# Chain banks of the first four gate pairs copied whole to SBUF before VectorE adds their halves, and the fifth product in its wide form in every pair

## The chip, the cores and the metric

The kernel runs on one core of one Trainium2 chip. The metric is device time in microseconds (us) of one execution, and the median over several executions is compared. The engines of a core run side by side and each takes its instructions in order: PE (TensorE, matmuls), DVE (VectorE), ACT (ScalarE), POOL (GpSimd, here almost only an issuer of DMAs) and SP (an issuer of DMAs).

## The reference

A decoder trunk of two layers on 512 tokens of width 1024, in float32. Layer 0 mixes tokens with a short gated convolution, layer 1 with sliding-window attention. Both layers end with the same feed-forward block, and the change lies there:

```python
D_MODEL, SEQ, D_FF = 1024, 512, 2816

def swiglu(h, w_gate_up, w_down):
    g, u = jnp.split(h @ w_gate_up, 2, axis=-1)
    return (jax.nn.silu(g) * u) @ w_down

def reference(x, ...):
    h = x
    for l in range(2):
        ...                                   # token mixing of the layer
        ff = swiglu(rmsnorm(h, ffn_pre_norm[l]), ffn_w_gate_up[l], ffn_w_down[l])
        h = h + rmsnorm(ff, ffn_post_norm[l])
    return h
```

## The kernel before

**Precision.** Every float32 operand is split into a high part (`hi`, a copy rounded by ACT) and a low part (`lo = x - hi`, by DVE), and a product is hi·hi + hi·lo + lo·hi on PE. So each weight tile of 128x1024 costs one ACT copy (`whi`, line L479) and one DVE subtraction (`wlo`, L480). Some weight tiles are sums of others that DVE adds first (L467).

**Stages.** The 22 column blocks of 128 of the gate and up matrices are taken in pairs. The first two blocks are computed plainly; the other 20 are ten *gate pairs*, numbered q = 0 to 9. Each pair is a 2x2 block product done with seven products instead of eight, and its jobs run in the order 1, 2, 6, 5, 7, 3, 4. After pairs 2, 4, 6 and 9 a stage of the down projection follows, also in the seven-product form; the first of these, after pair 2, is called down stage 0, and its first three jobs d0, d1 and d2 here.

**Chains.** PSUM has eight banks of 128x512. Products 1, 6, 7 and 4 add up in one pair of banks, the chain X (tile `gx`). After each of them `take` reads the running sum out before the next of the four may write: into `st` after 1, 6 and 4, and added to `u` after 7. Product 5 goes to chain Z (`gz`), product 2 to Y (`gy`), product 3 to Z as well or to a bank V of its own (`gv`).

**Wide and narrow.** A wide product has one 128x512 matmul for hi·(hi and lo) and one 128x256 matmul for lo·hi in each step, so each of its two banks holds two halves that must still be added: the first half by an ACT copy of 128x256, the second by a DVE addition that reads PSUM. A narrow product has three 128x256 matmuls in each step and one bank. Before, product 5 is narrow in pairs 0 and 1 (`FIVE = 2`), where it shares the one bank of Z with product 3, and wide from pair 2 on.

**Order.** The jobs stand in one list. After job j has been issued, `in_line` prepares job j + 3: ACT's `whi`, then DVE's `wlo`. So on DVE and ACT the reading-out of a product, the splitting of weights for three jobs later, and the splitting of the activations of the pair before (`s`, `ahi`, `alo`, L590 to L601) alternate in one fixed order:

```python
        for j, job in enumerate(jobs):
            if job.run:
                job.run(job)            # PE's matmuls, then take()
            prepare(j + LINE_LEAD)      # LINE_LEAD = 3: whi, wlo, then the sum for j + 4
            ...
                    late.pop(0)()       # a piece of the activations' splitting
            late += job.then() or [] if job.then else []   # after product 3: ACT's Silu
```

Gate pairs 0 to 2 and down stage 0 have no other work between them.

Of the kernel before, what the change touches and what calls it, by code (L numbers as in the profile page):

```python
# [12 lines left out]
AF = mybir.ActivationFunctionType  # L13
# [28 lines left out]
WARM = 9  # L42
LEAD = 2
LINE_LEAD = 3
FIVE = 2

EARLY_IN, REST_IN = 2, 0
ORDER = (
# [27 lines left out]
def yoco_kernel(  # L76
# [22 lines left out]
    nc = tc.nc  # L99
# [15 lines left out]
    def name(s):  # L115
        uid[0] += 1
        return f"{s}_{uid[0]}"

    def slot(s, dt=F32, w=S):
        return big.tile([P, w], dt, tag="slot", name=name(s), padded_shape=[P, S])  # L120

    def wide(s, dt=F32):
        return wides.tile([P, D], dt, tag="wide", name=name(s))
# [7 lines left out]
    def bank(s, pool=None):  # L131

        if pool is None:
            pool = (ps_mm, ps_sc, ps_mm, ps_pt)[turn[0] % 4]
            turn[0] += 1
        return pool.tile([P, S], F32, tag="bank", name=name(s))
# [56 lines left out]
    def mm3(out, whi, wlo, xhi, xlo, start, stop, **kw):  # L193
        nc.tensor.matmul(out, whi, xlo, start=start, stop=False, **kw)  # L194
        nc.tensor.matmul(out, whi, xhi, start=False, stop=False, **kw)  # L195
        nc.tensor.matmul(out, wlo, xhi, start=False, stop=stop, **kw)  # L196
# [256 lines left out]
    class Job:  # L453
# [10 lines left out]
        def add(self):  # L464
            if self.make:
                raw = self.raws[0].tile
                nc.vector.tensor_tensor(out=raw, in0=raw, in1=self.raws[1].tile, op=ALU.add)  # L467
# [203 lines left out]
    with tc.manual_schedule(engines=ALL):  # L671
# [52 lines left out]
        v = small.tile([P, 4], F32, tag="v", name=name("v"))  # L724
# [15 lines left out]
    both = []  # L740
# [84 lines left out]
    with tc.manual_schedule(engines=ALL):  # L825
# [21 lines left out]
        pools = {"p": ps_pt, "m": ps_mm, "s": ps_sc}  # L847
# [134 lines left out]
    def ffn(l, before, ahead, gain, gpres, following):  # L982
# [20 lines left out]
        def gate_jobs(q, factors, out, to, then):  # L1003

            sums = sums_of[f"g{l}{q}"]
            a21, a22, a11, a12 = (Raw(b) for b in sums.blocks)
            s1, s3, *rest = (Raw(b) for b in sums.sums)
            raws = {1: [a11], 2: [a12], 5: [s1], 7: [s3], 4: [a22]}  # L1010
            if rest:
                raws[6], raws[3] = ([r] for r in rest)
            else:
                raws[6], raws[3] = [a11, s1], [a12, a11]
            five = q >= FIVE
            broad = "XZ" if five else "X"
            chain = {1: "X", 6: "X", 7: "X", 4: "X", 5: "Z", 3: "V" if five else "Z", 2: "Y"}
            pools = {"X": ps_mm, "Y": ps_pt, "V": ps_pt, "Z": ps_sc}
            split = {}
            if q == 0:  # L1020

                pools = {"X": ps_sc, "Y": ps_pt, "V": ps_pt, "Z": ps_mm}
                raws[1], raws[2] = [], []
                split = {1: ahead.ready[4], 2: ahead.ready[5]}
            banks, kept = {}, []

            def tiles(a):
                return a.rearrange("p (e c) -> p e c", e=2)

            def take(p):  # L1030
                x, y, z, v = (banks.get(c) for c in "XYZV")
                st, u, gr = kept
                g0, g1 = (gr.rearrange("p (e h c) -> p e h c", e=2, h=2)[:, :, h]
                          for h in range(2))

                def add(out, a, b):
                    nc.vector.tensor_tensor(out=out, in0=a, in1=b, op=ALU.add)  # L1037

                if p == 2:
                    add(g0, tiles(y), tiles(st))  # L1040
                elif p == 5:
                    if not five:
                        nc.scalar.activation(u, z, AF.Copy)
                        return
                    for e in range(2):
                        ue = u[:, e * 256 : (e + 1) * 256]
                        nc.scalar.activation(ue, z[e][:, :256], AF.Copy)
                        add(ue, z[e][:, 256:], ue)
                    add(st, u, st)
                elif p == 3:  # L1050
                    add(g1, tiles(v if five else z), tiles(st))
                else:
                    for e in range(2):
                        a, b = x[e][:, :256], x[e][:, 256:]
                        ste, ue = (v[:, e * 256 : (e + 1) * 256] for v in (st, u))
                        if p == 7:
                            add(ue, a, ue)
                            add(ue, b, ue)
                            continue
                        nc.scalar.activation(ste, a, AF.Copy)  # L1060
                        add(ste, b, ste)
                if p == 4:
                    for g, m in ((g0, st), (g1, u)):
                        nc.vector.scalar_tensor_tensor(out=g, in0=tiles(m), scalar=-1.0, in1=g,
                                                       op0=ALU.mult, op1=ALU.mult)

            def run(p):
                def products(job):
                    if not kept:
                        kept.extend([slot("st"), slot("st"), wide("gr")])  # L1070
                    whi, wlo = split[p] if p in split else job.w
                    c = chain[p]
                    opened = c not in banks
                    if opened:
                        banks[c] = ([bank("g" + c.lower(), pools[c]) for _ in range(2)]
                                    if c in broad else bank("g" + c.lower(), pools[c]))
                    steps = [(e, k, slice(e * S + k * P, e * S + (k + 1) * P))
                             for e in range(2) for k in range(4)]
                    kw = {"skip_group_check": True}
                    if c in broad:  # L1080
                        for e, k, kk in steps:
                            nc.tensor.matmul(banks[c][e], whi[:, kk], factors[p][k][2],  # L1082
                                             start=opened and k == 0, stop=False, **kw)
                        for e, k, kk in steps:
                            nc.tensor.matmul(banks[c][e][:, :256], wlo[:, kk], factors[p][k][0],  # L1085
                                             start=False, stop=k == 3 and p in (4, 5), **kw)
                    else:
                        for e, k, kk in steps:
                            mm3(banks[c][:, e * 256 : (e + 1) * 256], whi[:, kk], wlo[:, kk],
                                *factors[p][k][:2], opened and e == k == 0,  # L1090
                                e == 1 and k == 3 and p in (2, 3), **kw)
                    take(p)
                return products

            def gate():
                nc.scalar.activation(kept[2], kept[2], AF.Silu)  # L1096

            def end():
                late = out(kept[2], to)
                then()  # L1100
                return late

            return [Job(raws[p], run(p), {3: gate, 4: end}.get(p), len(raws[p]) > 1)
                    for p in (1, 2, 6, 5, 7, 3, 4)]
# [42 lines left out]
        with tc.manual_schedule(engines=ALL):  # L1147
# [5 lines left out]
            def then(hf, k):  # L1153
                if hf == 0 and k in (5, 6):
                    for b in ((0, 1), (2, 3))[k - 5]:
                        before.turn(b, (2,))
                if hf == 0 and k == 6:
                    for b in range(4):
                        before.turn(b, (3,))
                    for f in range(KT):  # L1160
                        before.split(0, f, 1)
                    for b in range(4):
                        before.keep(b, 1)
                if hf == 1 and k == 1:
                    factors.update(before.factors())
                if hf == 1 and k == 3:
                    sum_on(f"{l}f0")
# [10 lines left out]
            for rd, (f0, f1) in enumerate(ROUNDS):  # L1178
                last = rd == len(ROUNDS) - 1
                for f in range(max(f0, PLAIN), f1, 2):  # L1180
                    q = (f - PLAIN) // 2
# [135 lines left out]
    class Heads:  # L1317
# [115 lines left out]
        def out(self):  # L1433
            if self.t < BOTH:
                hi, lo = halves("ohl", F32R)
            else:
                hi, lo = slot("ohi", F32R), slot("olo", F32R)
            nc.scalar.activation(hi, self.po, AF.Copy)
            nc.vector.tensor_tensor(out=lo, in0=self.po, in1=hi.bitcast(F32), op=ALU.subtract)
            at.append((hi, lo))  # L1440
# [25 lines left out]
    with tc.manual_schedule(engines=ALL):  # L1466
# [20 lines left out]
        for hf in range(2):  # L1487
            c = slice(hf * 256, (hf + 1) * 256)
# [54 lines left out]
    with tc.manual_schedule(engines=ALL):  # L1543
        sum_on("a0")
        for i in range(KT + 2):
# [9 lines left out]
            for c in order.split():  # L1555
# [11 lines left out]
                if op == "g":  # L1567

                    u = 2 * (t - EARLY - 1) + n[0]
# [126 lines left out]
```

## Time and profile before

| | |
|---|---|
| median of 3 runs | 1015.99 us (1015.88 to 1016.23) |
| the profiled execution | 1015.87 us, span 1014.1 us |
| granted TensorE clock | 0.999 |
| PE busy | 1005.4 us, 99% |
| DVE busy | 888.1 us, 88% |
| ACT busy | 582.6 us, 57% |
| gate pairs 0, 1, 2 of layer 0 (at us) | 204.0, 223.8, 243.5; down stage 0 from 263.8 |
| the same of layer 1 | 701.5, 721.1, 740.9; down stage 0 from 761.3 |

The timeline and the stretches give microseconds from the start of the span. A row of the timeline has start, duration, engine, line, operation, output and inputs, and at its end in square brackets how long the engine sat idle before it and who ended that. Consecutive instructions of an engine overlap a little, so their distance is shorter than their duration.

### The profile page before, as it was taken

Reading aid. Unit: us, or ns where it says so; the run is one execution under the profiler, and the core shown is the slowest. Engines: PE = TensorE matmul, PEld = TensorE weight load, DVE = VectorE, ACT = ScalarE, POOL = GpSimd, SP = SyncE. Lnnn points to the kernel's source line nnn. Section 1 sums busy time; section 2 is a strip of 40 time slices with the busy share of each in tenths; the row PEclk is TensorE's granted clock in tenths of the full one; section 3 lists DMA queues with packets and bytes.
Section 4 is the critical chain, followed back from the end, with each engine's and each line's share of the span. In section 5 each row is a group of like instructions: output and inputs, shape, how many; then the busy total and the mean of one; then the engine's idle time right before and its main releaser. Section 6 shows DMA issues by size and latency. Waiting matters only on the chain.

```text
span 1014.1 us, 16099 instructions
## 1 busy us (share of the span) xinstructions
PE 1005.4 (99%) x5880; PEld 885.6 (87%) x5880; DVE 888.1 (88%) x1528; ACT 582.6 (57%) x1051; POOL 195.0 (19%) x259
## 2 busy tenths in 40 slices
PE   9999999999999999999999999999999999999997
PEld 7888888999889898898898888889988888989986
DVE  5766767899889999999888998778997999999996
ACT  7322444875656465566485786677656564645641
POOL 0443033102101011000032754231111010110001
PEclk9999999999999999999999999999999999999999
DMA  9897689549969789769504889976899576979742
GB/s 357 291 261 232 178 251 337 175 166 271 343 233 291 242 290 312 245 217 338 197 1 141 211 248 266 277 252 151 274 289 332 168 245 224 305 264 265 243 177 83
DMA packets 66575, 244.50 MB, mean 241 GB/s; under 512 B 7872, under 2 KB 8384, under 8 KB 54720
## 3 DMA queue, kind: packets, MB, share of 16 engines
q1 hardware_dynamic: 51328, 145.98, 38.8%
q0 software_dynamic: 14592, 96.48, 37.5%
q10 hardware_dynamic: 576, 1.02, 0.3%
q8 instruction: 46, 0.75, 0.3%
q14 instruction: 33, 0.27, 0.1%
HBM read 237.15 MB, written 102.76 MB: 335 GB/s over the span
## 4 chain that ended last, share of the span: by engine, by line
PE 93%; DVE 4%; issue 1%; ACT 1%; DMA 0%; DVEq 0%; ACTq 0%
PE gx L1082 13%; PE gx L1085 7%; PE pcub L195 4%; PE pcub L196 4%; PE pcub L194 4%; PE px L195 4%; PE px L194 4%; PE px L196 4%; PE pmix L196 3%; PE pmix L195 3%; PE pmix L194 3%; PE gz L1082 3%; PE pz L195 2%; PE pz L194 2%; PE pz L196 2%; PE gy L194 2%
## 5 line engine op out<-in xcount | busy, mean ns | idle before, releaser
L480 DVE TENSOR_TENSOR wlo<-raw,whi 128x1024 fp32r<-128x1024 f32 x225 | 274.5, 1224 | 30.8 <-ACT whi L479 30.7
L479 ACT ACTIVATE whi<-raw 128x1024 fp32r<-128x1024 f32 x225 | 233.4, 1051 | 97.8 <-DVE raw L467 28.7
L1082 PE MATMUL gx<-xt,whi 128*128 128x512 f32 x480 | 120.8, 394 | 0.4 <-DVE st L1037 0.4
L1082 PEld LDWEIGHTS gx<-xt,whi 128*128 128x128 f32 x480 | 86.2, 189 | 16.6 <-issue 0.8
L548 POOL DMA_DIRECT2D hsum<-in_w_gb_dram x96 | 62.8, 733 | 151.5 <-ACT whi L479 88.5
L548 POOL DMA_DIRECT2D hsum<-hsum x32 | 25.3, 792 | 292.9 <-ACT whi L479 201.1
L1037 DVE TENSOR_TENSOR st<-gx,st 128x256 f32<-128x256 f32 x200 | 77.5, 418 | 2.2 <-ACT st L1060 0.4
L1060 ACT ACTIVATE st<-gx 128x256 f32<-128x256 f32 x120 | 43.4, 380 | 61.0 <-PE gx L1085 57.3
L1085 PEld LDWEIGHTS gx<-xt,wlo 128*128 128x128 f32 x480 | 65.5, 190 | 4.7
L1085 PE MATMUL gx<-xt,wlo 128*128 128x256 f32 x480 | 66.9, 282 | 0.0
L1096 ACT ACTIVATE gr<-gr 128x1024 f32<-128x1024 f32 x20 | 21.2, 1062 | 59.0 <-DVE gr L1037 59.0
L195 PE MATMUL px<-whi,ahi 128*128 128x512 f32 x120 | 46.7, 389 | 0.0
L194 PE MATMUL px<-wlo,ahi 128*128 128x512 f32 x120 | 46.7, 389 | 0.0
L196 PE MATMUL px<-whi,alo 128*128 128x512 f32 x120 | 46.7, 389 | 0.0
L194 PE MATMUL gy<-xlo,whi 128*128 128x256 f32 x160 | 45.3, 283 | 0.0
L195 PE MATMUL gy<-xhi,whi 128*128 128x256 f32 x160 | 45.3, 283 | 0.0
L196 PE MATMUL gy<-xhi,wlo 128*128 128x256 f32 x160 | 45.3, 283 | 0.0
L548 POOL DMA_DIRECT2D hsum<-in_w_dn_dram x48 | 32.1, 779 | 46.4 <-ACT whi L479 36.3
L1082 PE MATMUL gx<-xhl,whi 128*128 128x512 f32 x160 | 39.9, 391 | 0.0
L184 DVE TENSOR_TENSOR wlo<-raw,whi 128x512 fp32r<-128x512 f32 x50 | 33.0, 699 | 6.9 <-ACT whi L183 5.2
L301 POOL TENSOR_TENSOR ur<-uv,mhalf 128x1 f32<-128x1 f32 x15 | 13.9, 928 | 122.4 <-DVE uv L297 122.2
L649 DVE TENSOR_TENSOR mix<-mix,px 128x512 f32<-128x512 f32 x54 | 34.9, 681 | 2.8 <-PE px L196 2.8
(312 smaller groups left out, 2994.6 us busy)
## 6 DMA issues: line engine op xcount, KB each, us to landing
hsum<-in_w_gb_dram POOLq DMA_DIRECT2D x96, 512.0 KB, 7.7
raw<-hsum SPq DMA_DIRECT2D x88, 512.0 KB, 8.1
raw<-in_w_gb_dram SPq DMA_DIRECT2D x60, 512.0 KB, 7.4
hsum<-in_w_dn_dram POOLq DMA_DIRECT2D x36, 512.0 KB, 8.3
raw<-in_w_dn_dram SPq DMA_DIRECT2D x32, 512.0 KB, 6.3
hsum<-hsum POOLq DMA_DIRECT2D x28, 512.0 KB, 5.8
raw<-in_w_in_dram SPq DMA_DIRECT2D x21, 512.0 KB, 7.3
hsum<-in_w_dn_dram POOLq DMA_DIRECT2D x12, 768.0 KB, 11.6
```

Of the source, the lines that this page charges most:

```text
L184: nc.vector.tensor_tensor(out=lo[:, c], in0=raw[:, c], in1=hi[:, c].bitcast(F32), op=ALU.subtract)
L194: nc.tensor.matmul(out, whi, xlo, start=start, stop=False, **kw)
L195: nc.tensor.matmul(out, whi, xhi, start=False, stop=False, **kw)
L196: nc.tensor.matmul(out, wlo, xhi, start=False, stop=stop, **kw)
L479: self.begun = nc.scalar.activation(hi[:, :n], raw, AF.Copy)
L480: nc.vector.tensor_tensor(out=lo[:, :n], in0=raw, in1=hi[:, :n].bitcast(F32), op=ALU.subtract)
L548: nc.gpsimd.dma_start(dst, src, max_dma_last_dim=4 * 4 * S, **kw))
L649: nc.vector.tensor_tensor(out=m, in0=m, in1=banks[bs][r], op=ALU.subtract if half else ALU.add)
L1037: nc.vector.tensor_tensor(out=out, in0=a, in1=b, op=ALU.add)
L1060: nc.scalar.activation(ste, a, AF.Copy)
L1082: nc.tensor.matmul(banks[c][e], whi[:, kk], factors[p][k][2], start=opened and k == 0, stop=False, **kw)
L1085: nc.tensor.matmul(banks[c][e][:, :256], wlo[:, kk], factors[p][k][0], start=False, stop=k == 3 and p in (4, 5), **kw)
```

## The change

`FIVE` is gone: product 5 is wide in all ten pairs, and product 3 always has its own bank V. A new constant `EVICT = 4` names the first pair that still reads the banks as before. In pairs 0 to 3 (both layers) ACT copies each bank of a wide product whole, 128x512, into a new SBUF slot `both`, and DVE then adds the two halves from there. For product 7, whose two halves DVE added to `u` straight from PSUM, there are now two ACT copies per pair as well.

```diff
-FIVE = 2
+EVICT = 4
...
-            five = q >= FIVE
-            broad = "XZ" if five else "X"
-            chain = {1: "X", 6: "X", 7: "X", 4: "X", 5: "Z", 3: "V" if five else "Z", 2: "Y"}
+            chain = {1: "X", 6: "X", 7: "X", 4: "X", 5: "Z", 3: "V", 2: "Y"}
...
+                def parts(banks, e):
+                    if q >= EVICT:
+                        return banks[e][:, :256], banks[e][:, 256:]
+                    c = slot("both")
+                    nc.scalar.activation(c, banks[e], AF.Copy)
+                    return c[:, :256], c[:, 256:]
+
+                def join(out, banks):
+                    for e in range(2):
+                        oe = out[:, e * 256 : (e + 1) * 256]
+                        a, b = parts(banks, e)
+                        if q >= EVICT:
+                            nc.scalar.activation(oe, a, AF.Copy)
+                            a = oe
+                        add(oe, b, a)
+
                 if p == 2:
                     add(g0, tiles(y), tiles(st))
                 elif p == 5:
-                    if not five:
-                        nc.scalar.activation(u, z, AF.Copy)
-                        return
-                    for e in range(2):
-                        ue = u[:, e * 256 : (e + 1) * 256]
-                        nc.scalar.activation(ue, z[e][:, :256], AF.Copy)
-                        add(ue, z[e][:, 256:], ue)
+                    join(u, z)
                     add(st, u, st)
                 elif p == 3:
-                    add(g1, tiles(v if five else z), tiles(st))
+                    add(g1, tiles(v), tiles(st))
+                elif p == 7:
+                    for e, (a, b) in enumerate([parts(x, e) for e in range(2)]):
+                        ue = u[:, e * 256 : (e + 1) * 256]
+                        add(ue, a, ue)
+                        add(ue, b, ue)
                 else:
...
-                        nc.scalar.activation(ste, a, AF.Copy)
-                        add(ste, b, ste)
+                    join(st, x)
```

The order on DVE in pair 1, from the end of product 6's reading-out to the weights split after product 7. Here `st_2238` and `st_2239` before are `st` and `u`, and so are `st_2248` and `st_2249` now. Before:

```order
L1037 TENSOR_TENSOR st_2238<-gx_2242,st_2238 128x256
L480 TENSOR_TENSOR wlo_2326<-raw_1994,whi_2325 128x1024
L594 TENSOR_TENSOR s_2236<-gr_2014 128x256
L595 SCALAR_TENSOR_TENSOR s_2236<-s_2235,gr_2014 128x256
L480 TENSOR_TENSOR wlo_2367<-raw_2076,whi_2366 128x1024
L601 TENSOR_TENSOR alo_2374<-s_2235,ahi_2373 128x512
L1037 TENSOR_TENSOR st_2239<-gx_2241,st_2239 128x256 x2
L1037 TENSOR_TENSOR st_2239<-gx_2242,st_2239 128x256 x2
L480 TENSOR_TENSOR wlo_2398<-raw_2105,whi_2397 128x1024
```

Now:

```order
L1035 TENSOR_TENSOR st_2248<-both_2336 128x256
L480 TENSOR_TENSOR wlo_2340<-raw_1994,whi_2339 128x1024
L594 TENSOR_TENSOR s_2246<-gr_2014 128x256
L595 SCALAR_TENSOR_TENSOR s_2246<-s_2245,gr_2014 128x256
L1035 TENSOR_TENSOR st_2249<-both_2372 128x256
L1035 TENSOR_TENSOR st_2249<-both_2375 128x256
L1035 TENSOR_TENSOR st_2248<-st_2249,st_2248 128x512
L480 TENSOR_TENSOR wlo_2380<-raw_2078,whi_2379 128x1024
L601 TENSOR_TENSOR alo_2387<-s_2245,ahi_2386 128x512
L1035 TENSOR_TENSOR st_2249<-both_2406,st_2249 128x256 x2
L1035 TENSOR_TENSOR st_2249<-both_2408,st_2249 128x256 x2
L480 TENSOR_TENSOR wlo_2415<-raw_2109,whi_2414 128x1024
```

Three additions for product 5 stand in front of `wlo`; the other additions read `both` instead of the bank. Pair 0 is the same in this respect; pairs 2 and 3 had the three additions before.

The order on ACT at the start of pair 0, from the end of the plain blocks' Silu to product 6. Before:

```order
L995 ACTIVATE gr_2002<-pgu_1648 128x512
L1060 ACTIVATE st_2012<-gx_2015 128x256
L1060 ACTIVATE st_2012<-gx_2016 128x256
L479 ACTIVATE whi_2037<-raw_1984 128x1024
L590 ACTIVATE a_414_2009<-gr_2002 128x256
L479 ACTIVATE whi_2072<-raw_1986 128x1024
L1060 ACTIVATE st_2012<-gx_2015 128x256
```

Now:

```order
L995 ACTIVATE gr_2002<-pgu_1648 128x512
L1041 ACTIVATE both_2033<-gx_2015 128x512
L1041 ACTIVATE both_2036<-gx_2016 128x512
L479 ACTIVATE whi_2039<-raw_1984 128x1024
L590 ACTIVATE a_414_2009<-gr_2002 128x256
L479 ACTIVATE whi_2074<-raw_1986 128x1024
L1041 ACTIVATE both_2099<-gx_2015 128x512
```

The copies of product 1 and product 6 are twice as wide and write `both` instead of `st`; they stand at the same places, ahead of the `whi` of the weights.

The order on ACT at the end of pair 2, around its Silu (L1096 before, L1101 now) and the reading-out of product 4. Before:

```order
L600 ACTIVATE ahi_2673<-gr_2240 128x512
L1096 ACTIVATE gr_2473<-gr_2473 128x1024
L1060 ACTIVATE st_2471<-gx_2474 128x256
L1060 ACTIVATE st_2471<-gx_2475 128x256
L479 ACTIVATE whi_2700<-raw_2562 128x1024
L479 ACTIVATE whi_2723<-raw_2565 128x1024
```

Now:

```order
L600 ACTIVATE ahi_2703<-gr_2250 128x512
L1101 ACTIVATE gr_2493<-gr_2493 128x1024
L1041 ACTIVATE both_2724<-gx_2494 128x512
L1041 ACTIVATE both_2727<-gx_2495 128x512
L479 ACTIVATE whi_2732<-raw_2586 128x1024
L479 ACTIVATE whi_2755<-raw_2589 128x1024
```

Here too only the two copies behind the Silu change. The orders on SP and POOL do not change at all, and on PE only product 5 of pairs 0 and 1 does: sixteen wide matmuls stand where twenty-four narrow ones stood.

More of the change, by code (lines that the diff above doesn't have):

```diff
@@ L1041, in take @@
                 elif p == 5:
-                    if not five:
-                        nc.scalar.activation(u, z, AF.Copy)
-                        return
-                    for e in range(2):
-                        ue = u[:, e * 256 : (e + 1) * 256]
-                        nc.scalar.activation(ue, z[e][:, :256], AF.Copy)
-                        add(ue, z[e][:, 256:], ue)
+                    join(u, z)
                     add(st, u, st)
                 elif p == 3:
-                    add(g1, tiles(v if five else z), tiles(st))
-                else:
[L1053 to L1060, printed above, removed]
-                        add(ste, b, ste)
+                    add(g1, tiles(v), tiles(st))
[4 more added lines that the diff above has]
+                        add(ue, b, ue)
+                else:
+                    join(st, x)
                 if p == 4:
@@ L1075, in products @@
                         banks[c] = ([bank("g" + c.lower(), pools[c]) for _ in range(2)]
-                                    if c in broad else bank("g" + c.lower(), pools[c]))
+                                    if c in "XZ" else bank("g" + c.lower(), pools[c]))
                     steps = [(e, k, slice(e * S + k * P, e * S + (k + 1) * P))
@@ L1079, in products @@
                     kw = {"skip_group_check": True}
-                    if c in broad:
+                    if c in "XZ":
                         for e, k, kk in steps:
```

## The prediction

> **What bounds the kernel now.** I read the page first. Its first part (busy time) and its fourth (the chain that ended last) name PE, and the list of PE's own waits is nearly empty.
>
> ```profile
> PE 1005.4 (99%) x5880; PEld 885.6 (87%) x5880; DVE 888.1 (88%) x1528; ACT 582.6 (57%) x1051; POOL 195.0 (19%) x259
> PE 93%; DVE 4%; issue 1%; ACT 1%; DMA 0%; DVEq 0%; ACTq 0%
> PE gx L1082 <- DVE st L1037: 0.4, 2, 0.2
> ```
>
> A shorter PE would shorten the kernel, but nothing here leaves PE much to win. DVE's 88% is an average, so next I read the stretches: gate pairs 0, 1 and 2 and down stage 0 of layer 0, one row each (length, then PE, PEld, DVE, ACT and POOL busy).
>
> ```profile
> 204.00:223.80 19.80, 19.80 (x138) 18.46 (x137) 17.83 (x30) 14.23 (x22) 1.82 (x3) 1.00 0.63 213
> 223.80:243.50 19.70, 19.70 (x138) 18.36 (x137) 19.56 (x32) 12.24 (x20) 4.45 (x7) 1.00 0.71 198
> 243.50:263.80 20.30, 20.09 (x130) 18.13 (x129) 20.13 (x34) 11.55 (x20) 3.66 (x6) 1.00 1.01 330
> 263.80:292.50 28.70, 28.70 (x129) 23.77 (x128) 22.86 (x31) 17.58 (x24) 3.40 (x5) 1.00 0.98 335
> ```
>
> Pair 0 leaves DVE 2 us free. Pair 1 leaves 0.14 and pair 2 0.17: both engines are full there. Down stage 0 has room again. The timelines of PE and DVE show how close DVE is to holding PE at the end of this stretch:
>
> ```profile
> 261.52 1.22 DVE L480 TENSOR_TENSOR wlo<-raw,whi 128x1024 fp32r<-128x1024 f32 x1
> 267.59 3.49 DVE L480 TENSOR_TENSOR wlo<-raw,whi 128x1024 fp32r<-128x1024 f32 x3
> 260.96 2.06 PE L1082 MATMUL gx<-xt,whi 128*128 128x512 f32 x8 [0.21 <-DVE st L1037]
> 263.81 0.40 PE L194 MATMUL px<-wlo,a 128*128 128x512 f32 x1
> 269.28 0.39 PE L194 MATMUL px<-wlo,a 128*128 128x512 f32 x1
> ```
>
> The third row is product 4 of pair 2, which waits until DVE has read product 7 out of chain X. The last two are the first matmuls of d0 and d2; each needs the whole `wlo` of its job. That of d0 was done at 261.52 + 1.22 = 262.74. That of d2, the first of the three, was done at 267.59 + 1.22 = 268.81. With 0.13 from a DVE end to PE's start (DVE's last addition before product 4 ended at 260.83 in the chain row below) d2 could have begun at 268.94: only 0.34 of room. Layer 1 repeats all this 497.46 us later.
>
> **The change, part by part.**
>
> *PE, product 5 wide in pairs 0 and 1.* Narrow and wide starts of chain Z and the product behind each, from PE's timeline and the chain (the first and the last three rows belong to the steps below):
>
> ```profile
> 260.39 0.44 DVE st L1037
> 232.13 0.28 PE L194 MATMUL gz<-xt,whi 128*128 128x256 f32 x1
> 235.00 2.01 PE L1082 MATMUL gx<-xt,whi 128*128 128x512 f32 x8
> 301.00 1.84 PE gz L1082 x8
> 303.80 1.84 PE gx L1082 x8
> 251.94 2.00 PE L1082 MATMUL gz<-xt,whi 128*128 128x512 f32 x8
> 254.81 2.11 PE L1082 MATMUL gx<-xt,whi 128*128 128x512 f32 x8
> 257.71 0.28 PE L194 MATMUL gv<-xlo,whi 128*128 128x256 f32 x1
> ```
>
> Narrow takes 235.00 - 232.13 = 2.87, wide 303.80 - 301.00 = 2.80: 0.07 each, four times. It lies ahead of a stretch that DVE comes to decide, so I count it as nothing (if DVE does not decide, 0.14 a layer).
>
> *The additions that stay.* Products 1, 6, 7, 4, and 5 in pairs 2 and 3, keep their DVE additions; one operand or both now come from SBUF. The groups by form give the price of both kinds, and of the ACT copies:
>
> ```profile
> L1037 DVE TENSOR_TENSOR st<-gx,st 128x256 f32<-128x256 f32 x200 | 77.5, 418 | 2.2 <-ACT st L1060 0.4
> L594 DVE TENSOR_TENSOR s<-gr 128x256 f32<-128x256 f32 x36 | 15.0, 417 | 0.0
> L1060 ACT ACTIVATE st<-gx 128x256 f32<-128x256 f32 x120 | 43.4, 380 | 61.0 <-PE gx L1085 57.3
> ```
>
> L594 subtracts two halves of one SBUF tile, just what the new additions do: 417 ns against 418 from PSUM. I take no difference. [...]
>
> *X released by ACT.* PE no longer waits for DVE's additions there, only for two copies. This removes the 0.21 of idle at 260.96, with what the modelled ends hide: 0.38 in all (product 3 of pair 2, narrow, took 2.87 from 257.71 and was through at 260.58), and 0.07 before product 7 (254.81 - 251.94 - 2.80). What is late next is `wlo` of d0 and d2.
>
> *New DVE work.* In pairs 0 and 1 product 5 gets two additions of 128x256 and one of 128x512. In pair 2 they exist already:
>
> ```profile
> 256.81 0.75 DVE L1037 TENSOR_TENSOR st<-gz,st 128x256 f32<-128x256 f32 x2
> 257.59 0.69 DVE L1037 TENSOR_TENSOR st<-st,st 128x512 f32<-128x512 f32 x1
> 258.20 1.22 DVE L480 TENSOR_TENSOR wlo<-raw,whi 128x1024 fp32r<-128x1024 f32 x1
> ```
>
> 258.20 - 256.81 = 1.39 a pair, directly ahead of a `wlo`.
>
> *New ACT work.* A copy of a whole bank is priced by the narrow fifth product's copy; the next row shows that the instruction behind it follows 0.50 later:
>
> ```profile
> 207.63 0.67 ACT L1060 ACTIVATE st<-gx 128x256 f32<-128x256 f32 x2
> 208.16 1.08 ACT L479 ACTIVATE whi<-raw 128x1024 fp32r<-128x1024 f32 x1
> 215.39 0.60 ACT L1043 ACTIVATE st<-gz 128x512 f32<-128x512 f32 x1 [1.55 <-PE gz L196]
> 215.89 1.05 ACT L479 ACTIVATE whi<-raw 128x1024 fp32r<-128x1024 f32 x1
> 263.98 1.06 ACT L1096 ACTIVATE gr<-gr 128x1024 f32<-128x1024 f32 x1 [4.26 <-DVE gr L1037]
> 264.94 0.64 ACT L1060 ACTIVATE st<-gx 128x256 f32<-128x256 f32 x2
> ```
>
> A pair of copies took 208.16 - 207.63 = 0.53 and takes 1.00 now: 0.47 more, about 3 us a pair with the new copies for 7 and 5. ACT has 7 of 20 us free in each pair, so the cover is ACT's idle time. It matters only where DVE already waits for ACT, at these places:
>
> ```profile
> 208.50 0.75 DVE L1037 TENSOR_TENSOR st<-gx,st 128x256 f32<-128x256 f32 x2
> 209.28 1.23 DVE L480 TENSOR_TENSOR wlo<-raw,whi 128x1024 fp32r<-128x1024 f32 x1
> 215.41 0.41 DVE L595 SCALAR_TENSOR_TENSOR s<-s,gr 128x256 f32<-128x256 f32 x1
> 216.97 1.23 DVE L480 TENSOR_TENSOR wlo<-raw,whi 128x1024 fp32r<-128x1024 f32 x1 [1.14 <-ACT whi L479]
> 265.59 0.75 DVE L1037 TENSOR_TENSOR st<-gx,st 128x256 f32<-128x256 f32 x2
> 714.43 1.22 DVE L480 TENSOR_TENSOR wlo<-raw,whi 128x1024 fp32r<-128x1024 f32 x1 [1.15 <-ACT whi L479]
> ```
>
> *How far DVE falls behind in a layer.* In pair 0 the `wlo` at 209.28 began 0.04 after the `whi` that ended at 209.24, so it moves by 0.47. DVE then runs without a gap to 215.41; the new additions start at 215.41 + 0.47 + 0.33 (the distance from one such operation to the next: 0.75 for two less 0.42 for one) = 216.21, and the `wlo` behind them at 217.60 instead of 216.97: the 1.14 of idle takes up most, and 0.63 late is left. Pair 1 has no idle time: 0.63 + 1.39 = 2.02. Pair 2 adds no work, but the Silu waits for DVE and so moves by the same 2.02, to 266.00; the two copies of product 4 behind it end at 267.56 and 268.06, and DVE's second addition, due at 265.59 + 0.33 + 2.02 = 267.94, starts at about 268.08: 0.14 more, 2.16 in all.
>
> *The sum.* `wlo` of d2 is done at 268.81 + 2.16 = 270.97, and PE starts d2 at 271.10 instead of 269.28: 1.82 later. (d0 starts at 262.74 + 2.02 + 0.13 = 264.89, 1.08 later; d0 and d1 are through before 271.10, since they took 269.28 - 263.81 = 5.47.) Behind it the two `wlo` that follow at once, and DVE's idle time of down stage 0, bring DVE back ahead; PE has no free time in which it could catch up. Twice 1.82 is 3.6 us: 1015.87 + 3.6 = 1019.5. The profiled execution is 0.1 below the median, which I leave out.
>
> *What costs nothing.* Pair 3 follows down stage 0: DVE has pauses there, its product 5 was wide before, and PE's waits list has no entry in it; without that cover its longer copies could cost 0.2. Bank V in pairs 0 and 1 uses a bank that stood empty. SP and POOL keep their order; SP's loads wait until DVE has read a `raw` buffer and so go out up to 2 us later, but PE comes later by almost as much. The 512-wide slots for `both` are free when they are needed, since ACT's copies wait for nothing but PE (and ACT itself).
>
> **The rivals.**
>
> *First, not slower: additions from SBUF are shorter than those from PSUM.* Between product 5 of pair 0 and `wlo` of d2 there are 32 additions of this kind (8 in pair 0, 12 in pairs 1 and 2 each). At 68 ns less each (2.16 / 32) DVE is not late at all, and d2 starts at 268.94, 0.34 earlier: 1015.2. From 57 ns on (a lateness below 0.34) the kernel is not slower. Against it stand L1037 and L594 with 1 ns between them; for it, that no row shows exactly this instruction with cross-engine waits. The same result would follow if DVE's 0.63 and 1.39 met idle time that I take for busy, against 19.56 and 20.13 us busy in the two pairs. [...]
>
> *Second, slower still: ACT in line.* The new copies for 7 and 5 wait for PE and hold up the `whi` behind them; ACT also waits for DVE's sums (L467). If each of the five readings-out in pairs 1 and 2 delayed DVE by only a fifth of the 0.47 that the first one costs in pair 0, DVE would be 0.9 later: 2.8 a layer, 1021.4. Against it: once DVE is 2 us late, ACT is ahead of it by more than that.
>
> *Third, a real gain.* If DVE's lateness were absorbed wholly, PE would win 0.38 + 0.07 + 0.14 = 0.59 a layer, which gives 1014.7, still no difference that can be told.
>
> **How the numbers follow.** A change of 0.2% (2.0 us) is about what can be told from none. The forecast has 0.68; its own range goes from 1018.2 (pair 0 adds nothing: 1.53 late, 1.19 a layer) to 1020.6 (0.5 more a layer). The first rival has 0.19, the second 0.09, the third and anything better 0.04. The range reaches down to the first rival, 1015.2, and up to 1020.8. Slower: 0.68 + 0.09, less a little below the bound, 0.75. Same: 0.21. Faster: 0.04.
>
> **What would show it.** Right: in both layers DVE runs without a gap from product 5 of pair 0 to d2, pairs 0 and 1 have 1.3 to 1.4 us more DVE time each, PE's idle list shows `px` waiting for DVE's `wlo` (some 1 us at d0, 0.7 more at d2), no `gx` waits for DVE, and both layers lose the same, with nothing gained or lost elsewhere. Wrong: additions from `both` clearly under 417 ns, DVE idle in pair 1, or PE waiting for ACT.

## The result, and the profile after

| | before | after |
|---|---|---|
| median | 1015.99 us (1015.88 to 1016.23) | 1019.97 us (1019.53 to 1020.29) |
| profiled execution | 1015.87 us, span 1014.1 us | 1019.84 us, span 1018.1 us |

The change makes the kernel slower: a ratio of 1.0039 with a 95% interval of 1.0024 to 1.0053. The granted clock is 0.999 in both. The profiled executions differ by 3.97 us.

The first part of the page of after, and the whole list of PE's waits (for whom, then us in total, times and the longest):

```profile
PE 1006.4 (99%) x5848; PEld 884.2 (87%) x5848; DVE 894.7 (88%) x1540; ACT 602.3 (59%) x1071; POOL 194.7 (19%) x259
PE px L194 <- DVE wlo L480: 2.6, 4, 0.8
PE gv L196 <- DVE wlo L480: 1.1, 2, 0.6
PE idle L677 <- DVE ones L143: 1.1, 1, 1.1
```

No `gx` waits for DVE any more. Two other waits have come: four times at the first matmul of a down job, twice (once a layer) inside product 3 of pair 2 (0.57 us idle at 258.41 in layer 0), each time for a `wlo`. The timelines of PE and DVE give the places. First PE at the start of d0 and d2 in layer 0, then in layer 1:

```profile
264.94 0.50 PE L194 MATMUL px<-wlo,a 128*128 128x512 f32 x1 [0.85 <-DVE wlo L480]
271.13 0.50 PE L194 MATMUL px<-wlo,a 128*128 128x512 f32 x1 [0.44 <-DVE wlo L480]
764.36 0.50 PE L194 MATMUL px<-wlo,a 128*128 128x512 f32 x1 [0.84 <-DVE wlo L480]
770.55 0.50 PE L194 MATMUL px<-wlo,a 128*128 128x512 f32 x1 [0.45 <-DVE wlo L480]
```

And DVE in layer 0: the `wlo` behind product 1 of pair 0, the `wlo` behind product 5 of pairs 0 and 1 with the new additions, and the reading-out of product 4 of pair 2 ahead of the `wlo` of d2:

```profile
209.75 1.23 DVE L480 TENSOR_TENSOR wlo<-raw,whi 128x1024 fp32r<-128x1024 f32 x1 [0.45 <-ACT whi L479]
217.64 1.22 DVE L480 TENSOR_TENSOR wlo<-raw,whi 128x1024 fp32r<-128x1024 f32 x1
237.59 0.75 DVE L1035 TENSOR_TENSOR st<-both 128x256 f32<-128x256 f32 x2
238.38 0.69 DVE L1035 TENSOR_TENSOR st<-st,st 128x512 f32<-128x512 f32 x1
238.99 1.22 DVE L480 TENSOR_TENSOR wlo<-raw,whi 128x1024 fp32r<-128x1024 f32 x1
267.74 0.87 DVE L1035 TENSOR_TENSOR st<-both 128x256 f32<-128x256 f32 x2
269.86 3.49 DVE L480 TENSOR_TENSOR wlo<-raw,whi 128x1024 fp32r<-128x1024 f32 x3
```

The `wlo` of d2 begins 269.86 - 267.59 = 2.27 us later than before, and 1.22 later it is done at 271.08; PE starts at 271.13. The groups by form show the additions and the copies:

```profile
L1035 DVE TENSOR_TENSOR st<-both 128x256 f32<-128x256 f32 x64 | 24.9, 420 | 0.7
L1035 DVE TENSOR_TENSOR st<-gx,st 128x256 f32<-128x256 f32 x120 | 46.8, 419 | 1.6 <-ACT st L1049 0.4
L1041 ACT ACTIVATE both<-gx 128x512 f32<-128x512 f32 x64 | 34.6, 594 | 14.7 <-PE gx L1090 14.7
```

Where the 3.97 us lie can be read from one instruction that opens each part: the transposes of the normalised activations ahead of the feed-forward of layer 0, the attention of layer 1 and its feed-forward. Here the three of before, and then of after:

```profile
175.95 1.91 PE L339 MATMUL xt<-ident,xn 128*128 128x128 f32 x16
508.85 1.91 PE L339 MATMUL xt<-ident,xn 128*128 128x128 f32 x16
673.41 1.91 PE L339 MATMUL xt<-ident,xn 128*128 128x128 f32 x16
```

```profile
176.00 1.91 PE L339 MATMUL xt<-ident,xn 128*128 128x128 f32 x16
510.88 1.91 PE L339 MATMUL xt<-ident,xn 128*128 128x128 f32 x16
675.40 1.91 PE L339 MATMUL xt<-ident,xn 128*128 128x128 f32 x16
```

Feed-forward of layer 0: 332.90 before, 334.88 after, 1.98 more. From the third row to the end of the span 1014.1 - 673.41 = 340.69 and 1018.1 - 675.40 = 342.70: 2.01 more. The start and the attention differ by 0.05 or less. So each layer pays the same, and all of it in its feed-forward.

### The profile page after: what moved, and what is told of

Same layout as the page of the kernel before. It is cut to its first block, busy times and chain, and to the rows that moved or that the text cites. A ratio compares the mean times of both kernels' runs of the same rounds, so it can differ in the third digit from the quotient of the medians.

```text
span 1018.1 us, 16077 instructions
## 1 busy us (share of the span) xinstructions
PE 1006.4 (99%) x5848; PEld 884.2 (87%) x5848; DVE 894.7 (88%) x1540; ACT 602.3 (59%) x1071; POOL 194.7 (19%) x259
## 4 chain that ended last, share of the span: by engine, by line
PE 89%; DVE 8%; issue 2%; ACT 0%; DVEq 0%; ACTq 0%
PE gx L1087 12%; PE gx L1090 6%; PE pcub L194 4%; PE pcub L196 4%; PE pcub L195 4%; PE px L194 4%; PE px L195 3%; PE px L196 3%; PE gz L1087 3%; PE pmix L194 3%; PE pmix L195 3%; PE pmix L196 3%; DVE wlo L480 2%; PE pcub L709 2%; PE pz L194 2%
## 5 line engine op out<-in xcount | busy, mean ns | idle before, releaser
L1101 ACT ACTIVATE gr<-gr 128x1024 f32<-128x1024 f32 x20 | 21.2, 1062 | 52.0 <-DVE gr L1035 52.0
L1049 ACT ACTIVATE st<-gx 128x256 f32<-128x256 f32 x72 | 26.1, 379 | 38.5 <-PE gx L1090 36.4
L1035 DVE TENSOR_TENSOR st<-gx,st 128x256 f32<-128x256 f32 x120 | 46.8, 419 | 1.6 <-ACT st L1049 0.4
L196 PE MATMUL gv<-xhi,wlo 128*128 128x256 f32 x160 | 45.6, 285 | 1.1 <-DVE wlo L480 1.1
L194 PE MATMUL gv<-xlo,whi 128*128 128x256 f32 x160 | 45.3, 283 | 0.0
L195 PE MATMUL gv<-xhi,whi 128*128 128x256 f32 x160 | 45.3, 283 | 0.0
L1041 ACT ACTIVATE both<-gx 128x512 f32<-128x512 f32 x64 | 34.6, 594 | 14.7 <-PE gx L1090 14.7
```

The lines of the kernel that those rows point to most:

```text
L1041: nc.scalar.activation(c, banks[e], AF.Copy)
L1049: nc.scalar.activation(oe, a, AF.Copy)
```

## The experiments

Each kernel below is named by what it does. The length of layer 0's feed-forward (worked out as above, from each kernel's own trace) is given beside the median, since the part ahead of it varies from execution to execution, by up to 2.3 us in one profile. Each ratio is to the executions of before that were taken with that kernel (medians from 1015.99 to 1016.04).

| kernel | median us | ratio to before, 95% interval | feed-forward of layer 0, us |
|---|---|---|---|
| before | 1016.04 (22 runs) | | 332.90 |
| after | 1019.97 | 1.0039 [1.0024, 1.0053] | 334.88 |
| copies_only | 1016.47 | 1.0003 [0.9994, 1.0012] | 332.86 |
| wide_only | 1019.49 | 1.0034 [1.0021, 1.0046] | 334.47 |
| half_from_bank | 1021.53 | 1.0056 [1.0043, 1.0068] | 335.27 |
| one_more_add | 1021.15 | 1.0052 [1.0039, 1.0064] | 335.54 |
| first_as_before | 1019.48 | 1.0033 [1.0021, 1.0046] | 334.57 |
| five_on_pool | 1023.12 | 1.0070 [1.0058, 1.0083] | 336.50 |
| sums_on_pool | 1027.81 | 1.0115 [1.0100, 1.0131] | 339.04 |
| before_sums_on_pool | 1022.10 | 1.0065 [1.0052, 1.0077] | 336.36 |
| narrow_x | 1015.08 | 0.9990 [0.9981, 0.9999] | 332.45 |
| copies_6_7 | 1015.58 | 0.9994 [0.9985, 1.0003] | 332.63 |

### Which half of the change costs the time

*copies_only*: after, with the fifth product narrow again in pairs 0 and 1.

```diff
+FIVE = 2
-            chain = {1: "X", 6: "X", 7: "X", 4: "X", 5: "Z", 3: "V", 2: "Y"}
+            five = q >= FIVE
+            broad = "XZ" if five else "X"
+            chain = {1: "X", 6: "X", 7: "X", 4: "X", 5: "Z", 3: "V" if five else "Z", 2: "Y"}
...
+                    if not five:
+                        nc.scalar.activation(u, z, AF.Copy)
+                        return
...
```

> Undoes the wide fifth product of pairs 0 and 1 and keeps the whole-bank copies. Theory (VectorE is full from product 5 of pair 0 to d2, and its additions for the wide fifth product are what arrives at PE): VectorE's 0.47 us of pair 0 goes into the 1.14 of idle there, nothing is added in pair 1, 0.14 is left behind pair 2's Silu, so d2 may start at 268.81 + 0.14 + 0.13 = 269.08 instead of 269.28: 0.2 a layer less than before, 1015.6 us. Rival (ScalarE's longer copies, in line, carry the loss): most of the 4 us stays, 1018 to 1020.

*wide_only*: before, with `FIVE` at 0, so that the banks are read as before and the fifth product is wide everywhere.

```diff
-FIVE = 2
+FIVE = 0
```

> The wide fifth product alone, with the banks read as before. Theory: VectorE is about 0.1 late in pair 0 and 1.5 after pair 1, and product 4 of pair 2 still waits for VectorE's additions in chain X: 260.96 + 1.5 = 262.46, so d0 at 265.3 and d2 at about 270.9, 1.6 a layer: 1019.2 us, with gx waiting for DVE st in PE's list. Rival (ScalarE's longer copies carry the loss): about 1016.0.

The wide fifth product carries the loss: alone it makes the feed-forward 1.57 us longer and the kernel 1.0034 times as long (1019.49 us, 1019.2 expected), while the copies alone change nothing that can be told. On top of the wide product the copies add 0.41 to the feed-forward (334.88 against 334.47). PE's waits of copies_only and its first matmul of d2, and PE's waits of wide_only:

```profile
PE px L195 <- DVE wlo L481: 0.5, 2, 0.3
269.18 0.50 PE L195 MATMUL px<-wlo,a 128*128 128x512 f32 x1 [0.25 <-DVE wlo L481]
```

```profile
PE gx L1082 <- DVE st L1037: 2.2, 6, 0.7
```

With the copies, X makes nobody wait, and d2 starts where DVE lets it. With the additions alone, DVE is late as well, and PE meets the lateness at X instead of at the `px` of the down jobs. I had expected 1015.6 from copies_only; its feed-forward is 0.04 shorter than before and not 0.2. The reason shows in d2's row: PE stops there, and its first matmul after the stop takes 0.50 us instead of 0.39 (more below); d2's first twelve matmuls take 2.85 us here (269.18 to 272.03) and 2.72 in before.

### Whether DVE has any free time, and where X is released

*one_more_add*: after, with an addition of 128x512 in pair 1 that nobody reads.

```diff
                     add(st, u, st)
+                    if q == 1:
+                        add(slot("idle"), u, st)
```

> The changed kernel with one more VectorE addition of 128x512 behind product 5's in pair 1 of each layer (its result is not used). Theory: 0.61 to 0.7 us of VectorE work there arrives at d2 in full, 1.2 to 1.4 us in all: 1021.3. Rival (something else than VectorE's lateness sets the start of d0 and d2): no change, 1020.0.

*half_from_bank*: after, but DVE reads the second half of each bank from PSUM, the first from ACT's copy.

```diff
-                    return c[:, :256], c[:, 256:]
+                    return c[:, :256], banks[e][:, 256:]
```

> The changed kernel, but VectorE reads the second half of each bank from PSUM instead of from the copy; ScalarE's work is the same. Theory (an addition costs the same from either side): VectorE's order and times as in the changed kernel, but chain X is released by VectorE again, so product 4 of pair 2 starts 1.02 after product 7's additions begin, at 263.10, d0 at 265.95 and d2 at 271.4 to 271.5 instead of 271.13: 0.3 to 0.5 a layer more, 1020.7 us. [...]

The extra addition and the `wlo` behind it in one_more_add, and its d2:

```profile
239.38 0.69 DVE L1035 TENSOR_TENSOR idle<-st,st 128x512 f32<-128x512 f32 x1
239.99 1.22 DVE L480 TENSOR_TENSOR wlo<-raw,whi 128x1024 fp32r<-128x1024 f32 x1
272.13 0.50 PE L194 MATMUL px<-wlo,a 128*128 128x512 f32 x1 [0.45 <-DVE wlo L480]
```

It moves the `wlo` by 239.99 - 239.38 = 0.61 and lengthens the feed-forward by 0.66; the median rises by 1.18 for both layers. Added DVE time here becomes time of the kernel, about one for one. In half_from_bank X waits for DVE once more, and the additions with one operand in PSUM take as long as the others:

```profile
PE gx L1087 <- DVE st L1035: 2.3, 4, 0.7
L1035 DVE TENSOR_TENSOR st<-gx,both 128x256 f32<-128x256 f32 x48 | 18.5, 418 | 0.2
```

The list also names ACT's `whi` for four waits at X (1.1 us in all), ahead of product 4 of pairs 1 and 2 in both layers. In layer 0 the first matmul there begins 0.15 after the DVE addition that empties the first bank of X (244.01 to 244.16 in pair 1, 265.47 to 265.62 in pair 2), and the `whi` named is that of a later job. By these times they are DVE's releases as well. The feed-forward is 0.39 longer than that of after in layer 0 and, from the third row to the end, 0.58 in layer 1 (343.28 against 342.70). With both, 1020.9 us would follow, close to the 1020.7 expected. The median stands 0.6 above that; the profiled execution, the longest of the five (1023.22), had lost 2.3 us before the feed-forward began, which the edit doesn't touch.

### What the copies of product 1 cost

*first_as_before*: after, but product 1 of pair 0 is read as before.

```diff
+                old = q >= EVICT or (q == 0 and p == 1)
...
-                    if q >= EVICT:
+                    if old:
```

(the same in `join`)

> After, but product 1 of pair 0 alone is read out as before: two ACT copies of 128x256 and two VectorE additions that read PSUM, in both layers. Theory (the lateness of VectorE is a sum of steps, and the first of them is the 0.47 us by which the longer copies push the weights split behind them): wlo after product 1 starts 0.47 earlier than in after, but the idle time of pair 0 (1.14) takes up 1.39 only in part as before, so 0.47 less late at d2 in each layer: about 270.66 instead of 271.13, and 1019.97 - 0.94 = 1019.0 us in all. Rival (the first copies do not matter, because VectorE waits for ACT later in pair 0 in any case): d2 at 271.13 and 1020.0 us.

The `wlo` behind product 1, the reading-out of product 6 with the `wlo` behind it, the `wlo` behind product 5, and d2:

```profile
209.28 1.23 DVE L480 TENSOR_TENSOR wlo<-raw,whi 128x1024 fp32r<-128x1024 f32 x1
213.28 0.75 DVE L1035 TENSOR_TENSOR st<-both 128x256 f32<-128x256 f32 x2
214.10 1.23 DVE L480 TENSOR_TENSOR wlo<-raw,whi 128x1024 fp32r<-128x1024 f32 x1
217.31 1.22 DVE L480 TENSOR_TENSOR wlo<-raw,whi 128x1024 fp32r<-128x1024 f32 x1
270.80 0.50 PE L194 MATMUL px<-wlo,a 128*128 128x512 f32 x1 [0.46 <-DVE wlo L480]
```

The first `wlo` comes 0.47 earlier than in after, as worked out, but the one behind product 5 only 217.64 - 217.31 = 0.33, and the feed-forward is 0.31 shorter. The measured 1019.48 lies between the two expectations: in the trace two thirds of the term are there. The rest goes at the `wlo` at 214.10. It starts 0.82 after the additions ahead of it; in after that distance is 0.67 (213.76 to 214.43). In after ACT's `whi` for it ran from 213.05 to 214.11, behind the copies of product 6, and those had to wait for PE until 212.08. So DVE, being earlier, now waits about 0.15 for ACT, a wait that the profile doesn't mark.

### Two attempts to give DVE's work to GpSimd

*five_on_pool*: after, with the additions of product 5 in pairs 0 and 1 on GpSimd.

```diff
+                    eng = nc.gpsimd if p == 5 and q < 2 else nc.vector
+                    eng.tensor_tensor(out=out, in0=a, in1=b, op=ALU.add)
-                    nc.vector.tensor_tensor(out=out, in0=a, in1=b, op=ALU.add)
```

> The changed kernel with the three additions behind product 5 moved from VectorE to GpSimd in pairs 0 and 1. Theory: VectorE loses 1.39 us of work in each of the two pairs and is no later than with the copies alone (d2 at about 269.1); PE keeps that within 0.2 a layer of the kernel before: 1016.0 us. Rival (GpSimd and VectorE hinder each other in SBUF, both with two inputs there, or GpSimd's additions, about 0.7 us for 128x256 and 1.3 for 128x512 by its rows, come too late for product 7's): 1018 to 1020.

*sums_on_pool*: after, with the sums of weight tiles (L467 in after, L468 here) for pairs 1 and 2 on GpSimd. *before_sums_on_pool*: the same edit on before.

```diff
-                nc.vector.tensor_tensor(out=raw, in0=raw, in1=self.raws[1].tile, op=ALU.add)
+                eng = nc.gpsimd if self.pooled else nc.vector
+                eng.tensor_tensor(out=raw, in0=raw, in1=self.raws[1].tile, op=ALU.add)
...
+            for job in made:
+                job.pooled = q < 3
...
```

> The changed kernel with the sums of weight tiles for pairs 1 and 2 (four VectorE additions of 128x1024 in the stretch, 1.14 us each) on GpSimd. Theory: VectorE has 4.5 us less to do there and 2.2 us too much before, so it no longer holds PE, and PE also wins what it lost to chain X: 0.6 a layer under the kernel before, 1014.8 us. Rival (GpSimd needs about 2.6 us for each sum and makes whi late): PE waits for ACT whi or DVE wlo, 1016 to 1018.

> The kernel before with the same sums on GpSimd, banks read and product 5 as before. Theory: chain X and d2 wait for VectorE only because it is full, so without 4.5 us of its work PE is free too: 0.45 a layer under the kernel before, 1015.1 us. Rival (the waits at chain X come from the way the banks are read, by VectorE from PSUM): 1016.0.

All three came out slower, and the expectations missed by 7 to 13 us: their theories counted what DVE no longer does, but not what GpSimd does to DVE. For five_on_pool the rival named it, and priced it too low (1018 to 1020). GpSimd rows and the DVE rows beside them, first of five_on_pool, then of before_sums_on_pool, and last of sums_on_pool:

```profile
237.20 2.16 POOL L1036 TENSOR_TENSOR st<-both 128x256 f32<-128x256 f32 x2
239.44 1.36 POOL L1036 TENSOR_TENSOR st<-st,st 128x512 f32<-128x512 f32 x1
237.79 0.96 DVE L594 TENSOR_TENSOR s<-gr 128x256 f32<-128x256 f32 x1
239.57 2.31 DVE L480 TENSOR_TENSOR wlo<-raw,whi 128x1024 fp32r<-128x1024 f32 x1
```

```profile
251.19 2.98 POOL L468 TENSOR_TENSOR raw<-raw,raw 128x1024 f32<-128x1024 f32 x1
251.07 0.75 DVE L1038 TENSOR_TENSOR st<-gx,st 128x256 f32<-128x256 f32 x2
251.74 3.53 DVE L481 TENSOR_TENSOR wlo<-raw,whi 128x1024 fp32r<-128x1024 f32 x1
```

```profile
229.91 2.93 POOL L468 TENSOR_TENSOR raw<-raw,raw 128x1024 f32<-128x1024 f32 x1
230.00 3.47 DVE L1036 TENSOR_TENSOR st<-both 128x256 f32<-128x256 f32 x2
```

In these rows the DVE instructions with both operands in SBUF are longer beside a GpSimd addition: `wlo` takes 2.31 or 3.53 us instead of 1.22, L594 0.96 instead of 0.42, and two additions from `both` 3.47 instead of 0.75. The additions with one operand in PSUM, at 251.07, keep their 0.75 for two.

### Two versions meant to beat before

*narrow_x*: after, but products 1, 6, 7 and 4 of pair 1 are narrow.

```diff
+            broad = "Z" if q == 1 else "XZ"
...
+                elif p == 7 and q == 1:
+                    add(u, x, u)
+                elif q == 1:
+                    nc.scalar.activation(st, x, AF.Copy)
...
-                                    if c in "XZ" else bank("g" + c.lower(), pools[c]))
+                                    if c in broad else bank("g" + c.lower(), pools[c]))
...
```

> After, but in pair 1 products 1, 6, 7 and 4 are narrow (three 128x256 matmuls a step, one bank), so ACT's copy of one bank of 128x512 goes straight to st and VectorE adds no halves there; product 7 is one VectorE addition of 128x512 from PSUM. VectorE loses some 3 us of work in pair 1, PE gains 4 x 0.07 = 0.28 a layer. Theory (after is slower only because VectorE has no free time between product 5 of pair 0 and d2): VectorE is in time again, PE waits neither for wlo nor for X, and against before each layer wins 0.59 and loses 0.28: about 1015.4 us. Rival (PE's waits at d0 and d2 come from ACT's longer copies or from the loads, whatever VectorE does): still 1019 to 1020 us.

*copies_6_7*: before, with whole-bank copies for products 6 and 7 of pair 2 alone.

```diff
+                        if q == 2 and p in (6, 7):
+                            both = slot("both")
+                            nc.scalar.activation(both, x[e], AF.Copy)
+                            a, b = both[:, :256], both[:, 256:]
...
```

> Before, but ACT copies the whole banks of products 6 and 7 of pair 2 alone, in both layers; nothing is added on VectorE. Theory: X is released by ACT ahead of products 7, 3 and 4 of pair 2, where before lost 0.38 + 0.07 a layer; VectorE keeps its times, so d2 cannot start before 268.94 + 0.2: 0.15 to 0.3 earlier than before a layer, 1015.4 to 1015.7 us in all, at the edge of what can be told from 1016.0. Rival (copies of a whole bank hold VectorE up where it has no free time): 1016.5 to 1018 us, with PE waiting for wlo at d2 longer than 0.3.

PE at d2, its first two rows with the weight load (PEld) of the first, of narrow_x, and then of copies_6_7:

```profile
268.74 0.19 PEld L194 LDWEIGHTS px<-wlo,a 128*128 128x128 f32 x1
268.96 0.39 PE L194 MATMUL px<-wlo,a 128*128 128x512 f32 x1
269.19 0.39 PE L195 MATMUL px<-whi,a 128*128 128x512 f32 x1
```

```profile
269.24 0.19 PEld L194 LDWEIGHTS px<-wlo,a 128*128 128x128 f32 x1 [0.46 <-DVE wlo L480]
269.24 0.50 PE L194 MATMUL px<-wlo,a 128*128 128x512 f32 x1
269.57 0.39 PE L195 MATMUL px<-whi,a 128*128 128x512 f32 x1
```

narrow_x has no wait of PE left in the feed-forward and is the fastest of all, 0.45 ahead of before in the feed-forward of layer 0; the interval of its ratio ends just below 1. So with some 3 us of DVE work out of pair 1 the wide fifth product and the other copies cost nothing. By itself narrow_x does not part DVE from ACT, since it also takes five of ACT's eight copies of X out of pair 1. That the loss in after is DVE's lack of time and not ACT rests on copies_only, which keeps all eight and loses nothing that can be told, and on one_more_add, which adds to DVE alone. copies_6_7 takes away the X waits, but DVE still bounds d2; it is 0.27 ahead in the feed-forward of layer 0, as expected, which the medians can't tell from nothing.

## Why the prediction was right

*What bounds, and where the loss sits.* Right. PE stays at 99%, and the loss is its new wait for `wlo` at d0 and d2. one_more_add shows DVE as the cause, and narrow_x, wide_only and copies_only fit it. The prediction did not have the wait inside product 3 of pair 2 (0.57 in layer 0). It costs nothing more: PE is through with d1 at 270.54 even so (its last matmul starts at 270.31, and they come 0.23 apart), and DVE lets d2 start only at 271.13.

*How far DVE falls behind.* The steps were forecast at 209.75, 217.60, 264.89 (d0) and 271.10 (d2), and were measured at 209.75, 217.64, 264.94 and 271.13, in an execution that began the feed-forward 0.05 later. The additions of product 5 in pair 1 take 238.99 - 237.59 = 1.40, against 1.39. The 2.16 of lateness at d2 became 2.27 - 0.05 = 2.22. The step at product 4 was forecast at 0.14; the pair of additions at 267.74 takes 0.87 instead of 0.75.

*The 0.63 of pair 0.* Its size is right. Its working adds in full the 0.47 that the copies of product 1 cost, and that holds in part: with product 1 read as before, first_as_before gets 0.33 back, since the weights behind product 6's copies then hold DVE up.

*The term that was mis-sized.* "Twice 1.82 is 3.6 us" was measured as 1.98 + 2.01 = 3.99 for the two feed-forwards. The start of d2 was 1.85 later in layer 0, 1.80 without the 0.05 of the start, as worked out, but what follows d2 was not simply shifted by that: after the stop PE's first matmuls come 0.33 apart and then 0.24, where an uninterrupted stream has 0.23 (269.24 to 269.57 against 268.96 to 269.19 above). d2's first twelve matmuls took 2.87 in after (271.13 to 274.00) and 2.72 before (269.28 to 272.00). The sum had no term for this 0.15 a layer. Two smaller slips change nothing: ACT's free time in pair 0 is 5.6 us and not 7 (19.80 less 14.23), and the upper end of the forecast's own range adds up to 1020.5, not 1020.6.

*The rivals.* The first fell: no run shows the 57 to 68 ns that it needed. Additions from `both` take 420 ns and those from PSUM 419 in the same execution, and half_from_bank's, with one operand in each, 418; it was slower than after with X waiting for DVE again. The second, ACT in line, fell too: from 213.42 on DVE of after has no row with marked idle time up to d2, and the one short wait for a copy that shows is the 0.12 at product 4; PE's list has no wait for ACT, and copies_only loses nothing that can be told. The third fell for this change, though narrow_x shows that a gain of the size it named is there (0.45 in layer 0, with four narrow products that cost some 0.3) once DVE has the time.

## What to carry to other kernels

When two engines are both full in a stretch, read from the timeline how much room the second one has at the places where the first will wait for it (here 0.34 us at d2), and set every added instruction against that; the average of 88% says nothing on it. A wait that is removed on one path (here X) is worth no more than the room up to the next one. Before work is given to a third engine, look at where its operands and those of its neighbours lie (here a `wlo` of 1.22 us took 3.53 beside GpSimd).

## What the runs showed of the hardware that I had not expected

- A short stop of PE costs more than its idle time. The first matmul of d2 in after, behind 0.44 of idle time, takes 0.50 us instead of 0.39, and the next follows after 0.33 instead of 0.23, at a granted clock of 0.999. In narrow_x the weight load stands 0.22 ahead of its matmul; in copies_6_7, where the weights are what PE waits for, both begin at 269.24. It is not only a matter of late weights: in before a wait of PE for DVE's reading of chain X (0.21 idle) ends at 260.96, and there the weight load begins only 0.03 ahead, at 260.93, and the first matmul takes 0.47. So after a stop of either kind the load stood at most 0.03 ahead in these rows; that this is what makes the matmul slow is a reading of these rows, and no run took it apart.
- A GpSimd addition of 128x1024 took 2.98 us beside DVE against 1.22 on DVE (L467 in after), and in the same time held a `wlo` to 3.53 us. The copies of this change put more of DVE's additions in reach of that, as both operands now lie in SBUF: in sums_on_pool those from `both` took 582 ns on average instead of 420, while in before_sums_on_pool those from PSUM stayed at 419.
